# A grouped rms norm whose power is taken on a square of broadcast sums

## The chip, the cores and the metric

The kernel runs on one core of one Trainium2 chip. The metric is the device time of one execution in microseconds. Engines are named as in the profile: PE is TensorE (PEld its weight loads), DVE is VectorE, ACT is ScalarE, POOL is GpSimd, SP is SyncE, which issues most of the DMAs.

## The reference, cut to what matters

The program is a two-layer encoder over 1,024 tokens of width 1,024. Layer 0 is a gated long convolution, layer 1 a state-space mixer (SSD) with 2,048 inner channels. Near the end of layer 1 every token's 2,048 channels are normed in four groups of 512:

```
def rms_norm_groups(x, g, n_groups):
    shp = x.shape
    xf = x.astype(jnp.float32).reshape(shp[:-1] + (n_groups, shp[-1] // n_groups))
    xf = xf * lax.rsqrt(jnp.mean(jnp.square(xf), axis=-1, keepdims=True) + LN_EPS)
    return xf.reshape(shp) * g
...
    y = y_f + y_b + xs * d_skip.astype(jnp.float32)[:, None]
    y = rms_norm_groups(y.reshape(b, L, D_INNER) * jax.nn.silu(z), norm_g, SSD_GROUPS)
    return (y.astype(x.dtype) @ w_out).astype(x.dtype)
```

So each token has four reciprocal square roots, one for each group, and each of them scales 512 channels.

## The kernel before

Layer 1 (`ssd`) works on chunks of 128 tokens, for four groups: 32 pairs of group `g` and chunk `c`. Channels lie on the partitions and tokens along the free dimension: the tile `y` of a pair is 128 partitions x 4 blocks x 128 tokens. `ssd_forth` makes one pair: it loads, forms the forward half, adds the backward half that `ssd_back` has written to DRAM, multiplies by the gate `sz`, norms and stores `y` to `yt`. While group `n` goes forth, the backward pass of group `n + 1` goes on in the same steps (`ssd_back`), for the first three groups; beside the last group runs the first part of the output product (`Out.steps`).

Both are Python generators. `advance` steps a `Pipe`, and between two steps `fill` issues a share of the long matmul streams: the input projection (line 763) and later the output product (line 1203). A `yield` in a task so places its next instructions behind that share on each engine's in-order queue. W1 = 1 and W2 = 1 are such yields in the norm; W3 = 0.

The norm of a pair stands in lines 1143 to 1160:

- ACT squares `y` into `sq` (line 1143; the tile is named dwh or dwl in the trace), POOL adds its four blocks down to one (lines 1146, 1147).
- After a yield, PE multiplies `sq` by one column of ones (line 1151): the sum of each token comes out with tokens on the partitions, 128 x 1. DVE takes the mean and adds epsilon (line 1153), POOL raises it to the power -0.5 (line 1154), ACT scales the identity by it (line 1156), which makes a diagonal matrix `rs`.
- After another yield, PE multiplies a square of ones by the diagonal (line 1159): the 128 factors lie now along the free dimension, equal on all partitions. DVE multiplies `y` by them out of PSUM (line 1160), and SP stores `y`.

The four PSUM banks of `self.bank()` (tile `f` in the trace) are used in turn by all small products. POOL also does these in the same stage, in order: the descriptors of the `er` loads (line 1050), `dm` = identity times a column (line 1081), `m` + `dm` (line 1086), each for `ssd_back`. PE's product in line 1099 reads `m`, and line 1073 reads `er`. The tile `rs` has two buffers, shared with a scratch tile of `ssd_back` (line 1064). `norm`, the layer norm of the output, takes the same power on 128 x 1 (lines 1187, 1188).

Of the kernel before, what the change touches and what calls it, by code (L numbers as in the profile page):

```python
# [21 lines left out]
F32 = mybir.dt.float32  # L22
F32R = mybir.dt.float32r
AF = mybir.ActivationFunctionType
ALU = mybir.AluOpType
# [6 lines left out]
EPS = 1e-5  # L32
# [160 lines left out]
class Build:  # L193
# [914 lines left out]
    def ssd_forth(self, p, t, yt, sz, g, c, state):  # L1108

        nc, tt = self.nc, self.nc.vector.tensor_tensor  # L1110
        cs = slice(128 * c, 128 * c + 128)
        bc, xs = self.ssd_load(p, t, g, c, 1)
        if c:
            ec = self.ssd_decay(p, t, g, c, 0)
        yield
        if c < 7:
            xw = self.ssd_weigh(p, t, g, c, 0, xs)

        y = None

        def load():

            v = self.values(p, "s0", 2) if g == 3 and c % 5 > 2 else self.values(p, "y", YBB)
            nc.sync.dma_start(out=v, in_=t["ybd"][g, c])
            return v.rearrange("p (i n) -> p i n", i=4)
        if (g, c) in t["there"]:
            y = load()
        yield
        if c:
            y1 = self.ssd_offset(p, g, c, state, bc, ec)  # L1130
        if c < 7:
            self.ssd_update(p, t, g, c, 0, state, bc, xw)
        if y is None:
            while (g, c) not in t["there"]:
                yield
            y = load()
            for _ in range(W0): yield
        if c:
            (nc.gpsimd if g in YBG else nc.vector).tensor_tensor(out=y, in0=y, in1=y1, op=ALU.add)
        tt(out=y, in0=y, in1=sz[g][:, :, cs], op=ALU.mult)  # L1140

        sq = self.ht.tile([128, 512], F32, name=("dwh", "dwl")[(c + g) % 2]).rearrange("p (i n) -> p i n", i=4)
        nc.scalar.activation(sq, y, AF.Square)
        blocks = 4 if g in SQ else 1
        if blocks == 1:
            nc.gpsimd.tensor_tensor(out=sq[:, :2], in0=sq[:, :2], in1=sq[:, 2:], op=ALU.add)
            nc.gpsimd.tensor_tensor(out=sq[:, 0], in0=sq[:, 0], in1=sq[:, 1], op=ALU.add)
        for _ in range(W1): yield
        ps = self.bank()[:, :1]
        for i in range(blocks):  # L1150
            nc.tensor.matmul(ps, sq[:, i], t["one"][:, 0:1], start=i == 0, stop=i == blocks - 1)
        ss = p.tile([128, 1], F32, name="ss", bufs=1)
        nc.vector.tensor_scalar(out=ss, in0=ps, scalar1=1.0 / 512, scalar2=EPS, op0=ALU.mult, op1=ALU.add)
        nc.gpsimd.tensor_tensor(out=ss, in0=ss, in1=self.mhalf, op=ALU.pow)
        rs = p.tile([128, 128], F32, name="rs", bufs=2)
        nc.scalar.activation(rs, self.ident, AF.Copy, scale=ss)
        for _ in range(W2): yield
        ps = self.bank()[:, :128]
        nc.tensor.matmul(ps, t["one"], rs, start=True, stop=True)
        tt(out=y, in0=y, in1=ps.unsqueeze(1).broadcast_to([128, 4, 128]), op=ALU.mult)  # L1160
        for _ in range(W3): yield
        nc.sync.dma_start(out=yt[4 * g:4 * g + 4, :, cs].rearrange("b p t -> p b t"), in_=y)
        t["gone"].add((g, c))
# [386 lines left out]
```

## Time and profile before

| | |
|---|---|
| median of 3 runs | 2164.39 us (2164.05 to 2165.11) |
| profiled execution, own time | 2173.37 us |
| its span, first to last instruction | 2171.6 us |
| granted TensorE clock, mean | 0.987 |
| PE / DVE / ACT / POOL busy, share of the span | 96% / 72% / 52% / 15% |
| shares of the chain that ended last | PE 74%, DMA 11%, DVE 8%, ACT 3%, issue 2%, POOL 1% |

Shares of the span are means over both layers. The 32 norms lie between 1500 and 2110 us of the span, and what matters for them is read there. A duration is that of one instruction as the profiler saw it; the idle time of an engine is put down to what ended it.

### The profile page before, as it was taken

To read this page: it belongs to the slowest core of one execution; us is meant where nothing else is said; L and a number is where in the kernel's file an instruction comes from. 1 tells how busy PE (TensorE), PEld (TensorE's weight loads), DVE (VectorE), ACT (ScalarE), POOL (GpSimd) and SP (SyncE) were. 2 spreads that over 40 slices of the span, in tenths; PEclk is the share of its full clock that TensorE was granted. 3 is DMA by queue.
4 is the path that set the end of the run, shared out by engine and by line. 5 is a ranking of instruction groups with operands and counts; after the bars stand their busy time and mean duration, and the time that the engine had idled before them with its cause. 6 is when DMAs were issued, how large, how long until landed. Compare 5 with 4: busy or idle time off the path is not lost.

```text
span 2171.6 us, 28748 instructions
## 1 busy us (share of the span) xinstructions
PE 2089.6 (96%) x9930; PEld 1661.5 (77%) x9930; DVE 1567.9 (72%) x2268; ACT 1136.4 (52%) x1665; POOL 324.8 (15%) x385
## 2 busy tenths in 40 slices
PE   7999999999999999999999998999999999989897
PEld 5777777888888888888777776776777777767676
DVE  7999977676777777767766564664777777667575
ACT  4787866465656556556544343554455555432231
POOL 0000000000000000000000101244344344433120
PEclk9999999999999999999999999999999999989998
DMA  6277887665656556556776325343454555557652
GB/s 208 103 237 249 266 263 240 202 197 168 199 165 186 171 159 194 182 181 197 270 275 217 121 66 157 110 122 119 124 154 150 168 160 162 161 172 245 229 174 93
DMA packets 269631, 391.92 MB, mean 180 GB/s; under 512 B 31767, under 2 KB 168727, under 8 KB 268845
## 3 DMA queue, kind: packets, MB, share of 16 engines
q1 hardware_dynamic: 255741, 382.99, 55.8%
q0 software_dynamic: 13744, 7.09, 1.4%
q8 instruction: 79, 1.29, 0.2%
q14 instruction: 67, 0.55, 0.1%
HBM read 269.10 MB, written 120.85 MB: 180 GB/s over the span
## 4 chain that ended last, share of the span: by engine, by line
PE 74%; DMA 11%; DVE 8%; ACT 3%; issue 2%; SPq 1%; POOL 1%; POOLq 0%; DVEq 0%; ACTq 0%
PE pj L270 28%; PE pj L763 16%; PE pj L1203 8%; PE f L250 3%; PE f L252 3%; PE f L251 3%; DMA wr<-l_w_out 2%; PE f L1038 2%; PE pk L1203 2%; DMA tr<-y 2%; PE f L1015 1%; PE f L1099 1%; PE f L1073 1%; DMA bxd<-tr 1%; DVE wl L234 1%
## 5 line engine op out<-in xcount | busy, mean ns | idle before, releaser
L270 PE MATMUL pj<-xth,wh 128*128 128x512 f32 x1024 | 326.5, 398 | 1.8 <-ACT xth L233 1.8
L270 PE MATMUL pj<-xtl,wh 128*128 128x512 f32 x1024 | 326.5, 396 | 1.4 <-DVE xtl L234 1.4
L270 PE MATMUL pj<-xth,wl 128*128 128x512 f32 x1024 | 324.8, 394 | 0.0
L234 DVE TENSOR_TENSOR wl<-wr,wh 128x1024 fp32r<-128x1024 f32 x152 | 192.2, 1267 | 139.6 <-ACT wh L233 138.8
L233 ACT CAST wh<-wr 128x1024 fp32r<-128x1024 f32 x152 | 159.4, 1049 | 165.7 <-PE pj L1203 58.5
L270 PEld LDWEIGHTS pj<-xtl,wh 128*128 128x128 f32 x1024 | 192.7, 189 | 45.7 <-DVE xtl L234 2.4
L270 PEld LDWEIGHTS pj<-xth,wl 128*128 128x128 f32 x1024 | 193.0, 189 | 44.2 <-issue 0.5
L270 PEld LDWEIGHTS pj<-xth,wh 128*128 128x128 f32 x1024 | 189.4, 189 | 42.2 <-ACT xth L233 3.4
L763 PE MATMUL pj<-h1th,wh 128*128 128x512 f32 x640 | 212.8, 406 | 0.9 <-DVE cv L679 0.9
L763 PE MATMUL pj<-h1tl,wh 128*128 128x512 f32 x640 | 203.8, 395 | 0.0
L763 PE MATMUL pj<-h1th,wl 128*128 128x512 f32 x640 | 202.8, 394 | 0.0
L234 DVE TENSOR_TENSOR xl<-bs,xh 128x512 fp32r<-128x512 f32 x192 | 129.7, 687 | 51.9 <-ACT xh L233 51.1
L233 ACT CAST xh<-bs 128x512 fp32r<-128x512 f32 x192 | 117.8, 621 | 69.8 <-DMA bs<-vs 28.7
L763 PEld LDWEIGHTS pj<-h1th,wh 128*128 128x128 f32 x640 | 117.6, 189 | 38.6 <-issue 15.8
L567 DVE SCALAR_TENSOR_TENSOR cv<-pj,cw,cv 128x960 f32<-128x960 f32 x192 | 139.3, 745 | 4.9 <-ACT cv L564 2.8
L763 PEld LDWEIGHTS pj<-h1tl,wh 128*128 128x128 f32 x640 | 120.8, 189 | 26.9 <-issue 1.5
L763 PEld LDWEIGHTS pj<-h1th,wl 128*128 128x128 f32 x640 | 121.1, 190 | 25.7 <-issue 0.2
L1187 POOL TENSOR_SCALAR rs<-mv 128x1 f32<-128x1 f32 x16 | 6.3, 395 | 896.5 <-DMA yr<-y 707.9
L679 DVE SCALAR_TENSOR_TENSOR cv<-pj,cw,cv 128x1023 f32<-128x1023 f32 (+1 forms) x96 | 122.6, 1277 | 5.8 <-ACT cv L676 5.2
L1086 POOL TENSOR_TENSOR m<-m,dm 128x512 f32<-128x512 f32 x64 | 93.9, 1466 | 74.2 <-DVE m L1078 73.7
L1081 POOL TENSOR_TENSOR dm<-ident,dco 128x512 f32<-128x512 f32 x64 | 69.5, 1086 | 189.3 <-DVE dco L1066 137.2
L389 DVE TENSOR_TENSOR kr<-f,dec 64x512 f32<-64x512 f32 x128 | 87.9, 687 | 3.6 <-ACT dec L386 1.1
(292 smaller groups left out, 4195.4 us busy)
## 6 DMA issues: line engine op xcount, KB each, us to landing
wr<-w SPq DMA_DIRECT2D x104, 512.0 KB
k<-kd SPq DMA_DIRECT2D x256, 128.0 KB
wr<-l_w_out SPq DMA_DIRECT2D x64, 512.0 KB
ask<-asb SPq DMA_DIRECT2D x64, 256.0 KB
bs<-ask SPq DMA_DIRECT2D x64, 256.0 KB
kd<-asb SPq DMA_DIRECT2D x64, 256.0 KB
as<-asb SPq DMA_DIRECT2D x64, 256.0 KB
bs<-as SPq DMA_DIRECT2D x64, 256.0 KB
```

Of the source, the lines that this page charges most:

```text
L233: self.nc.scalar.copy(h, src)
L234: self.nc.vector.tensor_tensor(out=l, in0=src, in1=h.bitcast(F32), op=ALU.subtract)
L250: mm(out, ah, bh, start=start, stop=False)
L251: mm(out, ah, bl, start=False, stop=False)
L270: self.nc.tensor.matmul(ps[:, t], lhs[:, k], rhs[:, k, t], start=st, stop=sp)
L389: (nc.gpsimd if 2 * q + i in PM else nc.vector).tensor_tensor(out=ks[q ^ i][r], in0=ps[r], in1=dec[r], op=ALU.mult)
L567: nc.vector.scalar_tensor_tensor(out=acc[:, o], in0=ps[:, i], scalar=cw[:, w:w + 1], in1=acc[:, o], op0=ALU.mult, op1=ALU.add)
L679: nc.vector.scalar_tensor_tensor(out=acc[:, o], in0=ps[:, i], scalar=cw[:, w:w + 1], in1=acc[:, o], op0=ALU.mult, op1=ALU.add)
L763: nc.tensor.matmul(ps[:, c], lhs[:, k], rhs[k // 4][:, k % 4, c], start=st, stop=sp)
L1081: nc.gpsimd.tensor_tensor(out=dm, in0=self.ident.unsqueeze(1).broadcast_to([128, 4, 128]), in1=dco[:, h4:h4 + 4].unsqueeze(2).broadcast_to ...
L1086: nc.gpsimd.tensor_tensor(out=m, in0=m, in1=dm, op=ALU.add)
L1203: self.nc.tensor.matmul(po[hf], lhs[:, t], rhs[:, 512 * hf:512 * hf + 512], start=s, stop=e)
```

## The change

The first product swaps its operands: the square of ones becomes the stationary one and the 128 x 128 tile of squares the moving one. Its result has the same sum on all 128 partitions, tokens along the free dimension. DVE takes mean and epsilon on 128 x 128 instead of 128 x 1 and writes them to `rs` in SBUF; POOL takes the power on 128 x 128, in place, with the column of -0.5 broadcast along the free dimension. The diagonal (ACT) and the second product (PE) go, and the last multiply reads its factors from SBUF instead of PSUM. The yields stay where they were.

```
         for _ in range(W1): yield
-        ps = self.bank()[:, :1]
+
+        ps = self.bank()[:, :128]
         for i in range(blocks):
-            nc.tensor.matmul(ps, sq[:, i], t["one"][:, 0:1], start=i == 0, stop=i == blocks - 1)
-        ss = p.tile([128, 1], F32, name="ss", bufs=1)
-        nc.vector.tensor_scalar(out=ss, in0=ps, scalar1=1.0 / 512, scalar2=EPS, op0=ALU.mult, op1=ALU.add)
-        nc.gpsimd.tensor_tensor(out=ss, in0=ss, in1=self.mhalf, op=ALU.pow)
+            nc.tensor.matmul(ps, t["one"], sq[:, i], start=i == 0, stop=i == blocks - 1)
         rs = p.tile([128, 128], F32, name="rs", bufs=2)
-        nc.scalar.activation(rs, self.ident, AF.Copy, scale=ss)
+        nc.vector.tensor_scalar(out=rs, in0=ps, scalar1=1.0 / 512, scalar2=EPS, op0=ALU.mult, op1=ALU.add)
+        nc.gpsimd.tensor_tensor(out=rs, in0=rs, in1=self.mhalf.broadcast_to([128, 128]), op=ALU.pow)
         for _ in range(W2): yield
-        ps = self.bank()[:, :128]
-        nc.tensor.matmul(ps, t["one"], rs, start=True, stop=True)
-        tt(out=y, in0=y, in1=ps.unsqueeze(1).broadcast_to([128, 4, 128]), op=ALU.mult)
+        tt(out=y, in0=y, in1=rs.unsqueeze(1).broadcast_to([128, 4, 128]), op=ALU.mult)
         for _ in range(W3): yield
```

## Rows read from the trace of the kernel before

**Rows 1.** Windows: two stretches, busy us of each engine, clock, DMA share, GB/s.

```profile
1530.40:2000.00 469.60, 449.75 (x2336) 346.44 (x2332) 346.66 (x511) 222.97 (x302) 198.13 (x208) 0.98 0.54 166
2000.00:2104.70 104.70, 93.63 (x437) 74.94 (x434) 64.97 (x106) 26.45 (x40) 19.33 (x28) 0.97 0.66 210
```

**Rows 2.** Chain that ended last, 1755 to 1787 us: start us, us, what.

```profile
1763.92 0.12 PE f L1151 x2
1764.03 1.02 PE f L1099 x16
...
1773.99 0.22 PE f L1159 x2
1774.21 0.89 PE f L1038 x8
```

**Rows 3.** Single lines: ns min/median/max of one, first and last start, shape.

```profile
L1154 POOL TENSOR_TENSOR ss<-ss,mhalf x32: 547/558/1534, 1530.4 to 2104.7; 128x1 f32<-128x1 f32 x32
...
L1187 POOL TENSOR_SCALAR rs<-mv x16: 221/222/1080, 1098.6 to 2159.8; 128x1 f32<-128x1 f32 x16
...
L1146 POOL TENSOR_TENSOR dwh<-dwh x16: 728/1044/1612, 1507.4 to 2102.4; 128x256 f32<-128x256 f32 x16
...
L1147 POOL TENSOR_TENSOR dwh<-dwh x16: 456/466/887, 1508.4 to 2103.5; 128x128 f32<-128x128 f32 x16
```

**Rows 4.** Single lines again, the small instructions around the power.

```profile
L1153 DVE TENSOR_SCALAR ss<-f x32: 106/157/159, 1530.2 to 2104.5; 128x1 f32<-128x1 f32 x32
...
L1064 DVE SCALAR_TENSOR_TENSOR rs<-cbs,ident x32: 275/284/543, 1370.1 to 1984.4; 128x128 f32<-128x128 f32 x32
...
L1156 ACT ACTIVATE rs<-ident,ss x32: 384/401/404, 1531.0 to 2105.3; 128x128 f32<-128x128 f32 x32
```

**Rows 5.** Timeline: first and last power of the 32, and the multiply behind each.

```profile
1530.43 0.56 POOL L1154 TENSOR_TENSOR ss<-ss,mhalf 128x1 f32<-128x1 f32 x1 [1.39 <-DVE ss L1153]
...
1539.47 0.69 DVE L1160 TENSOR_TENSOR y<-y,f 128x512 f32<-128x512 f32 x1 [1.20 <-PE f L1159]
...
2104.70 0.55 POOL L1154 TENSOR_TENSOR ss<-ss,mhalf 128x1 f32<-128x1 f32 x1 [0.71 <-DVE ss L1153]
...
2106.27 0.69 DVE L1160 TENSOR_TENSOR y<-y,f 128x512 f32<-128x512 f32 x1 [0.45 <-PE f L1159]
```

**Rows 6.** Timeline of POOL, from one power to the next.

```profile
1764.43 0.56 POOL L1154 TENSOR_TENSOR ss<-ss,mhalf 128x1 f32<-128x1 f32 x1 [2.98 <-DVE ss L1153]
1767.73 1.19 POOL L1050 DMA_DIRECT2D er<-csd  x2 [2.74 <-PE f L1073]
...
1775.81 1.28 POOL L1086 TENSOR_TENSOR m<-m,dm 128x512 f32<-128x512 f32 x1
...
1785.54 0.56 POOL L1154 TENSOR_TENSOR ss<-ss,mhalf 128x1 f32<-128x1 f32 x1 [1.67 <-DVE ss L1153]
```

**Rows 7.** Timeline of POOL and of DVE, 1582 to 1587 us.

```profile
1582.30 3.36 POOL L1146 TENSOR_TENSOR dwl<-dwl 128x256 f32<-128x256 f32 x1 [0.69 <-ACT dwl L1143]
...
1582.06 1.21 DVE L234 TENSOR_TENSOR wl<-wr,wh 128x1024 fp32r<-128x1024 f32 x1
1583.18 0.68 DVE L1008 TENSOR_TENSOR xw<-bx,wdec 128x512 f32<-128x512 f32 x1
1583.78 0.68 DVE L1020 TENSOR_TENSOR s<-s,td 128x512 f32<-128x512 f32 x1
1584.38 0.68 DVE L1078 TENSOR_TENSOR m<-m,cbs 128x512 f32<-128x512 f32 x1
```

**Rows 8.** Single lines: two DVE instructions of one shape.

```profile
L1020 DVE TENSOR_TENSOR s<-s,td x48: 674/690/1796, 1381.0 to 2076.1; 128x512 f32<-128x512 f32 x48
...
L1021 DVE TENSOR_TENSOR s<-s,f x48: 666/680/691, 1405.8 to 2085.1; 128x512 f32<-128x512 f32 x48
```

**Rows 9.** Groups by line, 1500 to 2110 us: busy, mean ns, idle before, releasers.

```profile
L1073 PE MATMUL f<-er,eb 18*128 18x512 f32 x94 | 32.4, 511 | 19.0 <-DVE ss L1153 9.4 <-DVE y L1160 6.1 <-DVE y L1101 2.4
```

## Prediction

> **What bounds the kernel now.** I read the page first: PE is busy for 96% of the span and leads the chain that ended last, POOL is busy for 15%. Those are means over both layers, so I went to the stretch with the norms, by windows from the first power at 1530.4 us to the last at 2104.7 us [rows 1]. In the first 469.6 us, 23 pairs follow each other, 20.4 us apart; PE is busy 96%, DVE 74% (15.1 us of a pair) and POOL 42% (8.6 us). In the last 104.7 us, eight pairs are 13.1 us apart and DVE has 8.1 us of work in each. So PE leads, DVE has 5.3 us to spare per pair in the first stretch and 5.0 us in the second, and POOL has about 12 us in the first.
>
> The chain of waits shows what the norm costs the leading engine: 0.12 us for the narrow product and 0.22 us for the second one, once per pair; the diagonal and the power are not on it in this stretch [rows 2]. They are hidden, and the timeline shows by what: the first power starts at 1530.43 and the multiply that needs its result at 1539.47, because the yield puts other work of all engines in between; the last pair has 1.57 us from start to start [rows 5]. Over all 32 pairs the mean distance from the power's start to its multiply's start is 9.0 us in the first 24 and 6.4 us in the last eight.
>
> **What goes.** The second product: 0.22 us of PE on the chain. The diagonal: 0.40 us of ACT per pair [rows 4], 13 us in all, hidden already, since ACT is busy under half of the first stretch [rows 1]; uncovered it could give 0.4 us a pair, but only if the factors were waited for. One of the turns of the four PSUM banks goes too. PE idled ahead of line 1073, 9.4 us in all, until line 1153 had read its bank and 6.1 us until line 1160 had [rows 9]; the second kind can go, the first stays.
>
> **What grows a little.** The first product moves 128 columns instead of one. The second product has that shape, so it goes from 0.12 to 0.22 us [rows 2], and PE gains 0.12 us net per pair, 4 us over 32. DVE's mean and epsilon go from 0.157 us to about 0.28 us, the price of the only 128 x 128 DVE instruction here [rows 4]: 4 us in 32 pairs, inside DVE's spare time. The last multiply keeps its shape; reading both inputs from SBUF costs DVE nothing by itself (0.690 us against 0.680 us, medians) [rows 8]. The gain side is thus 4 us, with 6 us more if the bank waits go: some 4 to 10 us, as long as nothing waits for the factors.
>
> **What grows much: the power.** It goes from one element per partition to 128. No row shows a wide power. From below: POOL's adds take 0.456 us at 128 columns and 0.728 us at 256 (the shortest of each), so a further column of an add costs 2.1 ns [rows 3]; at that rate the power would take 0.558 + 127 x 0.0021 = 0.83 us. From above: a power on one column takes 0.558 us, while another POOL operation on the same 128 x 1 takes 0.222 us [rows 3]. The power's arithmetic on one column is therefore worth 0.336 us more than a plain one. If that is paid again for each column, the wide power takes 0.222 + 128 x 0.336 = 43.2 us. Taken against the add's line carried back to one column (0.456 - 127 x 0.0021 = 0.19 us), it would be 0.37 us a column and 47.6 us. The ends are far apart. I take 43.2 us: the nearest row is the power itself, and it shows a long chain of steps for a single column; nothing shows that columns overlap in it.
>
> The Trainium skill speaks for the lower end. "GPSIMD Engine Reference", section "Elementwise — side-by-side cycle accounting", gives a `tensor_tensor` add about 2.6 cycles per element on each core, a floor set by its two inputs and not by its arithmetic; the adds agree (2.1 ns), and for powers no run here shows it. If the power kept that rate too, the change would be worth what the third rival below says.
>
> **What 43.2 us does.** Nothing hides it. The multiply of line 1160 waits for it, and DVE is in order: behind it stand `ssd_back`'s `m` and `dco`, the evacuation of the projections and the squares' input of the next pair. On POOL, the `er` descriptors, the block adds and `m` + `dm` stand behind the power (the first of them 2.7 us after its end in one pair [rows 6]), and PE waits for `er`, `m` and the sums. POOL alone would need 8 + 43 = 51 us per pair against 20.4 us.
>
> Two sums bound the delay. If DVE runs on until the multiply, a pair loses the power less the distance that covers it: 24 x (43.2 - 9.0) + 8 x (43.2 - 6.4) = 1115 us. If DVE can do next to nothing while POOL computes, only its spare time covers: 24 x (43.2 - 5.3) + 8 x (43.2 - 5.0) = 1215 us. Rows speak for the second: a POOL add that needs 0.73 us took 3.36 us beside four DVE multiplies and subtractions with both inputs in SBUF and ended shortly after the last of these [rows 7, 3], and the DVE multiply with both inputs in SBUF has a longest time of 1.80 us while its like with one input in PSUM never exceeds 0.69 us [rows 8]. The Trainium skill ("SBUF — State Buffer", section "Who interferes with whom") calls this an exclusive lock for the whole instruction, whichever starts first; the 3.36 us agree, and by the rule alone the sum would be the 1215 us. But DVE instructions that read PSUM may go on, so I take the middle, 1165 us. The gain of 4 to 10 us is lost in this, since PE no longer leads. Against the profiled execution: 2173.4 + 1165 = 3338 us; the median of the runs lies 9 us under that execution, so 3330 us.
>
> **The rivals.** *Columns overlap in part.* If four columns are in flight, one costs 84 ns and the power 11 us: 24 x 2.0 + 8 x 4.6 = 85 us by the first sum, 24 x 5.7 + 8 x 6.0 = 185 us by the second, so about 2300 us. With two in flight it is 21.7 us, and about 2640 us. For it: POOL's adds overlap well. Against: the price of the single column.
>
> *The power fits in its cover.* At 5 to 6 us DVE's spare time is used up and the product's gain given back: about 2160 us, no change. That needs 40 ns a column, an eighth of the one-column price.
>
> *The power is nearly free, the kernel faster.* At 0.83 us to some 4 us, under 30 ns a column, all of it lies within the 9.0 us that cover it; PE keeps 4 us and up to 6 us of bank waits, and the shorter way to the factors may give a few more in the last stretch. That ends at 2150 us, between 2140 and 2160. For it: the add's slope; against it: 0.336 us for one column. The point from which it decides is 40 ns per column.
>
> **How the numbers follow.** About 0.2% (4 us) is what a measurement of this kernel tells from no change. Power paid column by column: 0.47, 3330 us, own range 2930 us (three quarters of the 0.336 us recurring, 32.5 us a power, first sum) to 3560 us (47.6 us a power, second sum, 1360 us, and a little for the hand-overs). Partly overlapped: 0.30, 2200 to 2930 us. Fits in its cover: 0.06. Nearly free: 0.17. So faster 0.17, same 0.06, slower 0.77. The range leaves out the nearly free case and a little above: 2160 to 3560 us, wide because one unknown price, multiplied by 128 columns and 32 pairs, decides all of it.
>
> **What the profile after would show.** POOL's line for the power with 32 instructions of some 43 us, and POOL the busiest engine from 1500 us on; pairs some 57 us apart; DVE's idle time ahead of line 1160 put down to POOL's power; PE's busy share in that stretch near 35%, its granted clock lower for want of work. Layer 0, before 1300 us, unchanged. A power of 10 us or less makes the forecast wrong in size, and one of 4 us or less wrong in sign. It would be wrong in another place if the power is long but the multiply does not wait, or if DVE stands still during it for no port's sake.

## Result and profile after

The changed kernel takes 2741.0 us (median of 4 runs, 2736.5 to 2745.9) against 2164.6 us for the kernel before: 1.266 times as long, 95% interval 1.2635 to 1.2691, or 576 us more. The forecast was 3330 us in a range of 2160 to 3560 us: the direction is right, the mechanism mostly, the size about twice too large.

First the windows, from the first power to that of pair 24 and on to that of pair 32 (columns as in [rows 1]):

```profile
1529.00:2419.70 890.70, 506.52 (x2296) 380.32 (x2292) 363.40 (x511) 214.17 (x279) 659.45 (x208) 0.76 0.29 88
2419.70:2661.20 241.50, 105.29 (x405) 81.95 (x402) 66.03 (x105) 23.92 (x32) 179.89 (x29) 0.70 0.28 90
```

The pairs are now 38.7 us apart in the first stretch and 30.2 us in the second, against 20.4 and 13.1 us [rows 1]. DVE and ACT have nearly as much to do as before; PE is busy for 612 us instead of 543 in about as many products, at a lower granted clock. POOL is busy 74% of both, DVE 41% and 27%, PE 57% and 44%; PE's granted clock of 0.76 and 0.70 is a mean over its two levels (1.2 and 2.4 GHz) in a stretch where it has often been idle. Nothing leads all the time: the engines take turns. Before 1500 us the two traces show the same work.

The single lines that answer to [rows 3], [rows 4] and the multiply of [rows 5] (ns min/median/max; then what ended the engine's idle time ahead of it, us and times):

```profile
L1155 POOL TENSOR_TENSOR rs<-rs,mhalf x32: 20717/20752/21735, 1529.0 to 2661.2; 128x128 f32<-128x128 f32 x32
...
L1154 DVE TENSOR_SCALAR rs<-f x32: 273/291/292, 1528.6 to 2660.8; 128x128 f32<-128x128 f32 x32
...
L1157 DVE TENSOR_TENSOR y<-y,rs x30: 683/693/1759, 1549.8 to 2682.0; 128x512 f32<-128x512 f32 x30
...
  POOL rs L1155: 580.5, 31
```

The wide power takes 20.75 us, not 43.2. And DVE stands idle for 580.5 us ahead of the multiply of line 1157, waiting for it: 31 times, 18.7 us each. That is the loss, to within 1%. One such wait in the timeline of DVE, and POOL beside it:

```profile
1777.46 0.29 DVE L1154 TENSOR_SCALAR rs<-f 128x128 f32<-128x128 f32 x1 [2.24 <-PE f L1152]
1798.62 1.53 DVE L1157 TENSOR_TENSOR y<-y,rs 128x512 f32<-128x512 f32 x1 [20.87 <-POOL rs L1155]
```

```profile
1777.83 20.75 POOL L1155 TENSOR_TENSOR rs<-rs,mhalf 128x128 f32<-128x128 f32 x1 [1.18 <-DVE rs L1154]
1798.57 1.03 POOL L1081 TENSOR_TENSOR dm<-ident,dco 128x512 f32<-128x512 f32 x1
1799.56 1.25 POOL L1050 DMA_DIRECT2D er<-csd  x2
...
1817.99 20.75 POOL L1155 TENSOR_TENSOR rs<-rs,mhalf 128x128 f32<-128x128 f32 x1 [4.40 <-DVE rs L1154]
```

DVE's next instruction after the sums is here the multiply itself, as in 13 of the 32 pairs. In the kernel before some ten DVE instructions lay between the two, which is how 9.0 us passed from power to multiply [rows 5]. The yield in the program is still there; what has changed is the order of DVE's queue, which is laid down when the program is built. Counted there (waits for semaphores left out), the multiply stands so many instructions behind the sums, pair by pair:

```
before  9 13 11 12 10 11 10 10 13 13 11 12 10 11 10  7  9 11 10 13 14 11 10  3  8  8  9  9  7  7  4  3
after   1  1  1 10  1  3  1  7 11  1  1 10  1  3  1  3  1  8 10  6  9  4  4  2  5  3  1  1  2  1 13  2
```

So the profile raises three questions: what a column of the power costs, how much of the loss is the multiply's early place on DVE, and what would remain without it.

### The profile page after: what moved, and what is told of

Same layout as the page of the kernel before. It is cut to its first block, busy times and chain, and to the rows that moved or that the text cites. A ratio compares the mean times of both kernels' runs of the same rounds, so it can differ in the third digit from the quotient of the medians.

```text
span 2743.0 us, 28549 instructions
## 1 busy us (share of the span) xinstructions
PE 2161.2 (79%) x9866; PEld 1707.4 (62%) x9866; DVE 1585.6 (58%) x2268; ACT 1124.4 (41%) x1633; POOL 966.2 (35%) x385
## 3 DMA queue, kind: packets, MB, share of 16 engines
q8 instruction: 78, 1.28, 0.2%
## 4 chain that ended last, share of the span: by engine, by line
PE 53%; POOL 26%; DVE 9%; issue 5%; DMA 4%; ACT 3%; SPq 0%; POOLq 0%; DVEq 0%; ACTq 0%
POOL rs L1155 24%; PE pj L270 24%; PE pj L763 9%; PE pj L1200 5%; PE f L250 2%; PE f L252 2%; PE f L251 2%; PE pk L1200 1%; DVE cv L679 1%; POOL m L1086 1%; DVE wl L234 1%; PE f L1073 1%; DVE m L1078 1%; PE f L383 1%; POOL dm L1081 1%
## 5 line engine op out<-in xcount | busy, mean ns | idle before, releaser
L1155 POOL TENSOR_TENSOR rs<-rs,mhalf 128x128 f32<-128x128 f32 x32 | 666.5, 20829 | 71.3 <-DVE rs L1154 71.3
L1157 DVE TENSOR_TENSOR y<-y,rs 128x512 f32<-128x512 f32 x30 | 26.3, 875 | 539.4 <-POOL rs L1155 539.4
L1073 PE MATMUL f<-er,eb 18*128 18x512 f32 x128 | 50.9, 558 | 265.6 <-DVE y L1101 126.0
L763 PE MATMUL pj<-h1th,wh 128*128 128x512 f32 x640 | 225.8, 430 | 0.9 <-DVE cv L679 0.9
L763 PE MATMUL pj<-h1tl,wh 128*128 128x512 f32 x640 | 214.4, 413 | 0.0
L763 PE MATMUL pj<-h1th,wl 128*128 128x512 f32 x640 | 211.5, 409 | 0.0
L1073 PEld LDWEIGHTS f<-er,eb 18*128 18x128 f32 x128 | 18.9, 203 | 297.2 <-DVE y L1101 130.9
L763 PEld LDWEIGHTS pj<-h1th,wh 128*128 128x128 f32 x640 | 125.6, 203 | 42.3 <-issue 17.4
L1077 ACT ACTIVATE m<-m 128x512 f32<-128x512 f32 x64 | 40.3, 631 | 267.6 <-DVE m L1076 267.2
L763 PEld LDWEIGHTS pj<-h1tl,wh 128*128 128x128 f32 x640 | 129.0, 202 | 30.6 <-issue 1.5
```

Source lines behind the costliest of these rows:

```text
L763: nc.tensor.matmul(ps[:, c], lhs[:, k], rhs[k // 4][:, k % 4, c], start=st, stop=sp)
L1073: nc.tensor.matmul(pe[d], t["eb"][g % 2][r, c // 2], er[r, h4:h4 + 4], start=True, stop=True)
L1077: nc.scalar.activation(m, m, AF.Exp)
L1155: nc.gpsimd.tensor_tensor(out=rs, in0=rs, in1=self.mhalf.broadcast_to([128, 128]), op=ALU.pow)
```

## The experiments

In each, "over" is the median less that of the kernel before on the same chip (2168 to 2171 us there).

### e1_widths: what a column costs

```
+            for n in (1, 2, 4, 8, 16, 32, 64, 128):
+                nc.gpsimd.tensor_tensor(out=wide[:, :n], in0=wide[:, :n], in1=self.mhalf.broadcast_to([128, n]), op=ALU.pow)
+            for n in (1, 2, 4, 8, 16, 32, 64, 128):
+                nc.gpsimd.tensor_tensor(out=wide[:, :n], in0=wide[:, :n], in1=self.mhalf.broadcast_to([128, n]), op=ALU.mult)
```

> The kernel before, with sixteen extra POOL instructions on a scratch tile in layer 0, where POOL has nothing to do: the power on 1, 2, 4, 8, 16, 32, 64 and 128 columns, then a multiply on the same widths. Theory (half of the one-column price is paid once, half per column): 0.40 us + 0.16 us per column, so 0.56, 0.72, 1.04, 1.68, 2.96, 5.5, 10.6 and 20.9 us. Rival (columns go in blocks, a block paid whole): flat at 0.56 us up to the block's width, then in steps. The multiplies: 0.19 us + 2.1 ns per column, 0.46 us at 128.

POOL's groups, with shapes kept apart:

```profile
L455 POOL TENSOR_TENSOR wide<-wide,mhalf 128x128 f32<-128x128 f32 x1 | 20.8, 20779 | 0.1
L455 POOL TENSOR_TENSOR wide<-wide,mhalf 128x64 f32<-128x64 f32 x1 | 10.5, 10521 | 0.1
L455 POOL TENSOR_TENSOR wide<-wide,mhalf 128x32 f32<-128x32 f32 x1 | 5.7, 5716 | 0.1
L455 POOL TENSOR_TENSOR wide<-wide,mhalf 128x16 f32<-128x16 f32 x1 | 2.9, 2895 | 0.1
L455 POOL TENSOR_TENSOR wide<-wide,mhalf 128x8 f32<-128x8 f32 x1 | 2.3, 2267 | 0.1
L455 POOL TENSOR_TENSOR wide<-wide,mhalf 128x4 f32<-128x4 f32 x1 | 1.0, 1019 | 0.1
L455 POOL TENSOR_TENSOR wide<-wide,mhalf 128x2 f32<-128x2 f32 x1 | 0.7, 712 | 0.1
L455 POOL TENSOR_TENSOR wide<-wide,mhalf 128x1 f32<-128x1 f32 x1 | 0.6, 597 | 0.1
L457 POOL TENSOR_TENSOR wide<-wide,mhalf 128x128 f32<-128x128 f32 x1 | 0.4, 399 | 0.1
```

From 1 to 128 columns the time grows by 20.18 us in 127 columns: 0.159 us each, and 0.160 us between 64 and 128. It is a line, not steps, as the theory had it; 8 columns lie 0.56 us above it, for a likely reason that the last section gives. About 0.4 us of the single-column price is paid once per instruction. A multiply of the same width takes 0.4 us.

### e2_cheap: the change without the price of the power

```
-        nc.gpsimd.tensor_tensor(out=rs, in0=rs, in1=self.mhalf.broadcast_to([128, 128]), op=ALU.pow)
+        nc.gpsimd.tensor_tensor(out=rs, in0=rs, in1=self.mhalf.broadcast_to([128, 128]), op=ALU.mult)
```

> The kernel after, with POOL multiplying by the column of -0.5 where it took the power (the norm's factors are wrong, all else is as in the change). Theory (the power's duration is all that costs): 4 to 10 us under the kernel before, 2155 to 2161 us. Rival (the new place of the last multiply on DVE or its two inputs in SBUF cost something by themselves): at or above 2165 us, up to 2200 us.

2165.0 us against 2169.0 us, ratio 0.9982 (0.9970 to 0.9993): 4 us under. The rest of the change is worth about what PE's side was said to give, 0.12 us a pair. DVE's queue has here the order of the kernel after, so that order costs nothing while the factors come soon. The bank waits ahead of line 1073 did not go, they moved:

```profile
L1073 PE MATMUL f<-er,eb 18*128 18x512 f32 x94 | 30.9, 505 | 17.6 <-DVE rs L1154 7.3 <-DVE y L1101 7.3 <-DVE y L1040 2.9
```

17.6 us of idle time against 19.0 us [rows 9], now for other readers of the banks.

### e5_cols32 and e5_cols64: a shorter power in place

```
-        nc.gpsimd.tensor_tensor(out=rs, in0=rs, in1=self.mhalf.broadcast_to([128, 128]), op=ALU.pow)
+        nc.gpsimd.tensor_tensor(out=rs[:, :32], in0=rs[:, :32], in1=self.mhalf.broadcast_to([128, 32]), op=ALU.pow)
```

> The kernel after with the power on the first 32 of the 128 columns only (the other 96 tokens of a chunk keep mean plus epsilon as their factor, so the norm is left out for them): 5.7 us a power. Theory (a pair loses the power less about 2.9 us, as the kernel after loses 17.8 of 20.75 us): 32 x 2.8 = 90 us over the kernel before, about 2255 us. Rival (a power of some 5 us fits in DVE's spare time): 2160 to 2175 us.

> The same with 64 columns (the norm is left out for 64 tokens of a chunk): 10.5 us a power. Theory: 32 x 7.6 = 243 us over the kernel before, about 2410 us. Rival (spare time of 5 us a pair covers): 32 x 5.3 = 170 us over, about 2335 us.

2271.4 us (over by 103 us, ratio 1.048, 1.046 to 1.049) and 2411.6 us (over by 243 us, ratio 1.112, 1.110 to 1.115). The power took 5.44 and 10.55 us, so a pair loses 3.2 and 7.6 us, and 18.0 us at 20.75: in each case the power less 2 to 3 us. A power of 5.4 us does not fit in DVE's spare 5.3 us; that rival fell.

### e9_order: the multiply back in its place on DVE

```
         for _ in range(W2): yield
-        tt(out=y, in0=y, in1=rs.unsqueeze(1).broadcast_to([128, 4, 128]), op=ALU.mult)
+        on = self.bank()[:, :1]
+        nc.tensor.matmul(on, self.ident, t["one"][:, 0:1], start=True, stop=True)
+        nc.vector.scalar_tensor_tensor(out=y, in0=y, scalar=on, in1=rs.unsqueeze(1).broadcast_to([128, 4, 128]), op0=ALU.mult, op1=ALU.mult)
```

> The kernel after, with the last multiply put back to its old place on DVE: behind the yield PE makes a column of ones in PSUM (identity times one column), and the multiply takes it as a third factor of 1.0. It then stands some 9 instructions behind the sums on DVE instead of right behind them; PE does not wait for the power. Theory (the lost cover is a good part of the loss): less than the kernel after, near the dead power's 411 us over the kernel before, so about 2580 us; with a cover of 9.0 and 6.4 us the arithmetic gives 400 us. Rival (POOL's queue alone sets the loss, wherever DVE waits): 2740 us, as the kernel after.

With the small product, which PE reaches only after its share of the projection, DVE's queue is again that of the kernel before (9, 13, 11, 12, 10, 11 instructions apart, and so on). 2616.6 us: over by 448 us, ratio 1.2064 (1.2044 to 1.2084). Putting the order back gives 128 of the 576 us. DVE's idle time ahead of the multiply:

```profile
L1159 DVE SCALAR_TENSOR_TENSOR y<-y,f,rs x30: 756/1210/2454, 1548.9 to 2552.9; 128x512 f32<-128x512 f32 x30
...
  POOL rs L1155: 447.8, 32
```

447.8 us of wait, 448 us of loss. The edit has a price of its own: the multiply with its third factor takes 1.21 us instead of 0.69 us (medians), some 17 us over 32 pairs, and PE waits 204 us ahead of line 1073 for line 1159 to free the bank of the small product. So the 128 us are what this edit gives; no run separates what the place alone is worth.

### e15_late2 and e16_late3: the multiply later still

e9_order with W2 = 2 and W2 = 3: one and two yields more. (The yields ahead of the sums, W1, are 2 in every kernel here, not 1.)

> The run with the multiply's old order put back (448 us over the kernel before), with one yield more ahead of the multiply: some 20 DVE instructions stand now between the sums and the multiply instead of some 10. Theory (the loss is DVE's wait at the multiply: 581 us of wait and 576 us of loss in the kernel after, 448 and 448 in that run): the wait falls by about 6 us per pair, to some 250 us, until POOL's own work (about 29 us a pair in the first stretch, 23 in the last) bounds it; so about 300 us over the kernel before, 2470 us. Rival (POOL's bare occupancy with its queue sets some 410 us, as the dead power does): 2575 us or more.

> The same with two yields more, some 30 DVE instructions in between. Theory: DVE hardly waits any more, and POOL's bare work is what is left: 24 x 8.5 + 8 x 10 = 285 us over the kernel before, about 2450 us, no less than with one yield more by much. Rival (as in the other run): 2575 us or more.

2463.8 us (over by 296 us, ratio 1.137, 1.134 to 1.139) and 2460.5 us (over by 292 us, ratio 1.136, 1.133 to 1.138), both near the theory's time, though the wait for the power in e15_late2 fell to 186 us and not to 250. In e16_late3 DVE waits 10.4 us in all for the power, and 36 us for the small product (what ended its idle time ahead of the multiply, us and times):

```profile
  PE f L1158: 36.0, 22
  POOL rs L1155: 10.4, 1
```

POOL's groups and its busy time say what is left (the first five numbers after the window are its length and the busy us of PE, PEld, DVE and ACT; POOL's follows):

```profile
L1155 POOL TENSOR_TENSOR rs<-rs,mhalf 128x128 f32<-128x128 f32 x32 | 667.1, 20846 | 13.2 <-DVE rs L1154 13.2
```

```profile
1529.00:2300.00 771.00, 560.05 (x2587) 426.98 (x2585) 368.79 (x566) 229.83 (x296) 740.74 (x221) 0.84 0.40 122
```

POOL is busy for 740.7 of 771 us, 96%, and has waited only 13 us ahead of its 32 powers. It is the bound: the pairs are 28.9 us apart in the first stretch and 24.2 in the second, about the sum of the power and POOL's other work.

### e3_dead and e8_oldpath: the wide power in the kernel before

e3_dead adds a wide power behind the narrow one, and nobody reads it:

```
         nc.gpsimd.tensor_tensor(out=ss, in0=ss, in1=self.mhalf, op=ALU.pow)
+        nc.gpsimd.tensor_tensor(out=sq[:, 2], in0=sq[:, 1], in1=self.mhalf.broadcast_to([128, 128]), op=ALU.pow)
```

> The kernel before with a second, wide power on POOL behind the narrow one, whose result nobody reads. POOL then has 8 + 21.3 us of work per pair against 20.4 us. Theory (POOL's bare work is one part of the loss, DVE standing at the multiply the other): 24 x 8.9 + 8 x 10.5 = 300 us over the kernel before, about 2465 us, and DVE not waiting ahead of the last multiply. Rival (DVE instructions with two inputs in SBUF are locked out while POOL computes): 500 us over, or more, and such DVE instructions ending only when the power ends.

2576.7 us, over by 408 us, ratio 1.188 (1.185 to 1.191). That is between the two expectations. POOL's bare work does not explain all of it: POOL is busy 89% of the first stretch and 83% of the second. Its queue is the likely reason for the surplus, though no run tests it alone: the next pair's narrow power stands behind the dead one, and ACT waits for it,

```profile
ACT rs L1157 <- POOL ss L1154: 473.6, 32, 38.5
...
PE f L1099 <- POOL m L1086: 138.8, 14, 18.9
```

(engine and line that waited, for whom, us in all, times, longest). The lock-out is refuted by the timeline of DVE during one dead power, which ran from 1668.48 us for 21.29 us:

```profile
1668.48 21.29 POOL L1155 TENSOR_TENSOR dwl<-dwl,mhalf 128x128 f32<-128x128 f32 x1
```

```profile
1666.97 1.23 DVE L1020 TENSOR_TENSOR s<-s,td 128x512 f32<-128x512 f32 x1
1668.46 0.69 DVE L1078 TENSOR_TENSOR m<-m,cbs 128x512 f32<-128x512 f32 x1 [0.27 <-ACT m L1077]
...
1679.52 0.68 DVE L1008 TENSOR_TENSOR xw<-bx,wdec 128x512 f32<-128x512 f32 x1
1680.11 0.68 DVE L1020 TENSOR_TENSOR s<-s,td 128x512 f32<-128x512 f32 x1
```

Lines 1008 and 1020 have both inputs in SBUF and take 0.68 us in the middle of the power, no more than in the kernel before [rows 7, 8]. So it is in all 32 dead powers: 92 instructions of lines 1008, 1020, 1078, 1139 and 1140 within them took 0.68 us in the median and at most 0.88 us. The same line 1020 beside a POOL add, at 1666.97, took 1.23 us.

e8_oldpath widens the narrow power itself and keeps the diagonal and the second product:

```
-        nc.gpsimd.tensor_tensor(out=ss, in0=ss, in1=self.mhalf, op=ALU.pow)
+        nc.gpsimd.tensor_tensor(out=sq[:, 1], in0=ss.broadcast_to([128, 128]), in1=self.mhalf.broadcast_to([128, 128]), op=ALU.pow)
...
-        nc.scalar.activation(rs, self.ident, AF.Copy, scale=ss)
+        nc.scalar.activation(rs, self.ident, AF.Copy, scale=sq[:, 1, 0:1])
```

> The kernel before with the power made 128 wide (the 128 x 1 sums broadcast; the diagonal takes column 0): the wide power stands on the path of the factors, but the diagonal, the second product and the place of the last multiply on DVE, some 9 instructions behind the sums, stay. Theory (the change also lost its cover, because the multiply moved up on DVE): the cover of 9.0 and 6.4 us holds, 24 x 11.8 + 8 x 14.4 = 400 us over the kernel before, about 2565 us. Rival (the order on DVE does not matter): 570 us over, about 2740 us, as in the kernel after.

2764.8 us, over by 596 us, ratio 1.275 (1.272 to 1.278): near the rival's number, but not for its reason. DVE's queue was the old one and DVE waited only 114 us ahead of the multiply. ACT waited 700 us for the power and PE 388 us for the diagonal: each is in order, and what stood behind them (evacuations, the projection) waited too. It took e9_order, in which neither waits for the power itself, to answer the question.

### e13_after_sq and e14_order_sq: the block adds out of POOL's queue

```
-SQ = ()
+SQ = (0, 1, 2, 3)
```

This setting lets PE sum the four blocks; e13 is the kernel after with it, e14 is e9_order with it.

> The kernel after, with the four blocks of squares summed by PE (four products into one bank, a setting that the kernel has) instead of being added on POOL first. POOL then has no block adds, and PE does not wait for adds that stand behind a power on POOL (156 us of PE's idle time in the kernel after). Theory (DVE at the multiply sets the loss, POOL's queue comes second): about 1.1 us of adds and at most a few us more per pair, 2680 to 2720 us. Rival (the queue behind the power is the first cause): 150 us less, about 2590 us.

> The same with the last multiply at its old place on DVE, as in the run with the order put back (448 us over the kernel before). What is left there is POOL's queue and the multiply's shorter wait. Theory (POOL's queue, adds behind the power among it, holds the rest): the power and POOL's other work bound a pair at 20.8 + 6.3 us in the first stretch, so some 60 to 120 us less than that run, 2500 to 2560 us. Rival (the multiply's wait alone holds the rest): no more than 30 us less, 2590 to 2620 us.

2811.2 us (ratio 1.296, 1.291 to 1.300) and 2629.4 us (ratio 1.212, 1.208 to 1.216): over by 640 and 458 us, that is 64 us more than without it, and 10 us more. All four expectations missed, the last by 9 us. Taking the adds off POOL shortened nothing, so they are not shown to be a cause; the setting also gives PE three more products a pair. PE's wait ahead of the sums went from POOL's adds (154 us in the kernel after) to ACT's squares (178 us in e13). In e13 DVE waited even longer at the multiply, 612 us, and POOL waited 174 us ahead of its powers for DVE's sums, where the kernel after has 71 us. That fits a loop in which the power and DVE's work follow each other.

### e6_lnexp: the factors by logarithm and exponential on ACT

```
-        nc.vector.tensor_scalar(out=rs, in0=ps, scalar1=1.0 / 512, scalar2=EPS, op0=ALU.mult, op1=ALU.add)
-        nc.gpsimd.tensor_tensor(out=rs, in0=rs, in1=self.mhalf.broadcast_to([128, 128]), op=ALU.pow)
+        nc.scalar.activation(rs, ps, AF.Ln, scale=1.0 / 512, bias=t["eps"])
+        nc.scalar.activation(rs, rs, AF.Exp, scale=-0.5)
```

> The kernel after, with DVE's mean and POOL's power replaced by two ACT instructions on 128 x 128: the logarithm of sum/512 + epsilon out of PSUM, then the exponential of -0.5 times it. Theory (only the price of the power is against the change, and ACT has room for 0.4 us and two table loads of 1.28 us more per pair): 4 to 10 us under the kernel before, 2155 to 2161 us. Rival (the table loads delay ACT's evacuations, and the projections wait): 10 to 40 us over.

2196.0 us, over by 28 us, ratio 1.0123 (1.0106 to 1.0140). ACT's table loads (line, count, busy us, mean ns):

```profile
L1156 ACT ACT_TABLE_LOAD x32 | 41.1, 1283 | 0.6
L1157 ACT ACT_TABLE_LOAD x32 | 41.1, 1283 | 0.6
L1079 ACT ACT_TABLE_LOAD x23 | 29.5, 1283 | 0.4
```

The logarithm and the exponential each load a table every time; line 1079, the exponential of `ssd_back`, saves 10 of its former 33. That is 54 more loads of 1.28 us, 69 us of ACT time. The time is within the rival's 10 to 40 us; that the loads cost the 28 us was not tested by itself. No version here that computes the norm beats the kernel before.

## Why the prediction was right in direction and wrong in size

| kernel | over, us | DVE idle ahead of the multiply for the power, us |
|---|---|---|
| e5_cols32, power 5.4 us | 103 | 110 |
| e5_cols64, power 10.6 us | 243 | 266 |
| after, power 20.75 us | 576 | 581 |
| e13, blocks summed by PE | 640 | 612 |
| e9, multiply in its old place | 448 | 448 |
| e14, the same, blocks summed by PE | 458 | 453 |
| e15, multiply one yield later | 296 | 186 |
| e16, two yields later | 292 | 10 |

**What goes: right.** 4 us of gain, the lower end of 4 to 10 (e2_cheap). The 6 us of bank waits did not come; that wait passed to other readers of the banks.

**The price of the power: the term that was mis-sized, and the step that failed.** "If that is paid again for each column" took all of the 0.336 us by which a one-column power exceeds a plain operation. Measured, 0.16 us recurs and the rest is paid once, so the power is 20.75 us instead of 43.2. One column cannot tell a fixed part from a recurring one; the prediction said so by its bounds, 0.83 and 47.6 us, and took the upper. The measured time lies in the range of its second case, "Partly overlapped" (0.30, 2200 to 2930 us), and not in that of the first (0.47).

The Trainium skill's 2.6 cycles per element of a `tensor_tensor` ("GPSIMD Engine Reference", section "Elementwise — side-by-side cycle accounting") hold for adds (2.1 ns a column [rows 3]), not for the power, whose column costs 75 times as much.

**The cover: also wrong, the other way.** With the right price the two sums give 24 x (20.75 - 9.0) + 8 x (20.75 - 6.4) = 397 us and 24 x (20.75 - 5.3) + 8 x (20.75 - 5.0) = 497 us, and the loss was 576 us. The cover that the prediction read from the timeline was there in the kernel before (9.1 us in the mean of the first 24 pairs by the trace, not 9.0) and did not survive the change: the multiply left its place behind ten DVE instructions once it no longer depended on a PE product. Of the 20.75 us, only 2 to 3 are covered. The prediction's last sign of being wrong came true: DVE stands still during the power "for no port's sake", since its next instruction waits for the power. So the two errors partly cancel, which is luck; the price alone, corrected, would have left the forecast too low.

**POOL's bare work: right, and the floor.** The prediction set it beside DVE's wait as "51 us per pair"; at the true price it is 29 us, and e16_late3 shows it as the bound, 292 us. So the 576 us divide, by these runs, into 292 us that POOL's time costs when the multiply stands late enough, 156 us more (448 - 292) because the old distance of some ten instructions is too short for 20.75 us, and 128 us because the change shortened that distance (the last two as far as e9_order's own price lets them be told apart).

**DVE held up by the port: wrong, though two rows pointed to it.** POOL's adds and DVE's two-input instructions hold each other up [rows 7, 8], but the power, once under way, does not hold up DVE. The Trainium skill's exclusive lock for the whole instruction ("SBUF — State Buffer", section "Who interferes with whom") is not what these traces show for a power of 21 us; the measurement decides. Only the power's start looks like such a lock (last section), and that is worth at most 1 us in a power.

**Of the rivals**, two columns in flight, 21.7 us and about 2640 us, came nearest to the power's time, without that mechanism being shown. That the power would fit in its cover, or be nearly free, was refuted in place at 5.4 us. The point from which the change would pay, put at 40 ns a column and 5 to 6 us, lies lower: at a power of some 2 us, an estimate from 5.44 us less the 3.2 us lost, to which no run went down.

## What to carry to other kernels

Price an operation at the width at which it will run: one column shows a fixed and a recurring part as one number, and a trial of the instruction at two widths separates them. Where a value is needed on all partitions, compute an expensive function on the narrow form and broadcast the result; here 128 x 1 and a second product cost PE 0.12 us a pair more than 128 x 128, and POOL 20 us less. A cover read from a trace belongs to the order of the queues that the trace had: when a dependency goes, look at the order of the program as built before counting on it.

## What the runs showed of the hardware, unexpected

A POOL power on 128 partitions costs 0.16 us for each column and about 0.4 us once, in a line from 1 to 128 columns (e1_widths). While it runs, DVE instructions with both inputs in SBUF keep their 0.68 us, whereas beside POOL adds the same line rose to 1.23 us and one add to 3.36 us [rows 7]. In these traces contention came with POOL's short adds, and with the long power at its start alone.

At the start it shows in the power's own time. The longest power of the kernel after, and the DVE instruction across its start:

```profile
1859.08 2.13 DVE L234 TENSOR_TENSOR wl<-wr,wh 128x1024 fp32r<-128x1024 f32 x1
1860.10 21.73 POOL L1155 TENSOR_TENSOR rs<-rs,mhalf 128x128 f32<-128x128 f32 x1
```

Line 234 has both inputs in SBUF and still had 1.11 us to run; the power took 0.98 us more than its 20.75 us. In the eight kernels with a power on 128 columns (after, e3, e8, e9, e13 to e16) 48 of 256 powers took over 20.85 us. Each of the 48 began with such a DVE instruction running, or within 0.02 us of one's start, and each took longer by what that instruction had left, less 0.13 to 0.18 us. DVE instructions that read PSUM across the start left the power at 20.7 to 20.8 us. In e3_dead one line 1008 ran across a start and was itself drawn out, to 1.46 us; that power took 20.75 us. The dead power shown above is one of the 48 (21.29 us, behind line 1078), and so, by its place, is the power on 8 columns: it began at 6.32 us in e1_widths, DVE's line 234 ran from 5.87 to 7.10 us, and it took 2.27 us where the line gives 1.71 us. Why the power is held up at its start and not later is not shown.
